# One ring of three buffers for the query weights and the second output projection, and the top-k ordered behind the second norm

## The chip, the core and the metric

The kernel runs on one core of one Trainium2 chip. A core has TensorE (PE, matrix products), VectorE (DVE), ScalarE (ACT), GpSimd (POOL) and SyncE (SP, which here only starts transfers). The metric is the device time of one execution in microseconds; lower is better.

## The reference, cut to what matters

```python
for l in range(DEPTH):                                    # DEPTH 1, x is (1, 512, 1024), f32
    proj = x @ w_in[l]                                    # 1024 -> 3072
    y_conv = gb * short_conv(gc * hc, conv_w[l], conv_b[l])
    y_att = rms_norm(diff_attention(q, k, v, lam), subln_g[l]) * (1.0 - lam_init)
    y_mix = jnp.concatenate([y_conv, y_att], axis=-1) @ w_out[l]
    x = layer_norm(DEEPNORM_ALPHA * x + y_mix, ln1_g[l], ln1_b[l])
    x = layer_norm(DEEPNORM_ALPHA * x + peer(x, ...), ln2_g[l], ln2_b[l])

def one_chunk(xc):                                        # in peer: 128 tokens
    q = (xc @ wq).reshape(128, 8, 2, 128)                 # 8 heads, two halves
    sc = jnp.einsum('chpd,hpnd->chpn', q, keys)           # 128 keys a half
    s1, i1 = lax.top_k(sc[:, :, 0], 16); s2, i2 = lax.top_k(sc[:, :, 1], 16)
    cand = s1[..., :, None] + s2[..., None, :]            # 256 candidates
    top_s, pos = lax.top_k(cand, 16)                      # 16 of 16384 experts a head
    g = jax.nn.softmax(top_s)
    act = jax.nn.gelu(jnp.einsum('chkd,cd->chk', u[eidx], xc))
    return jnp.einsum('chk,chkd->cd', g * act, v[eidx])
```

## The kernel before, in words

The 512 tokens are four chunks of 128. Every f32 weight block (128 x 1024, 512 KB) is loaded by SP's queue into a tile `raw` and split into a high part `whi` (a cast on ScalarE) and a low part `wlo` (a difference on VectorE or GpSimd); a product is then three matrix products, high by high, high by low and low by high (`mm3`, L89 to L91). `wblock` does the loading and splitting (L80 to L86), and its three tiles come from a pool: `raw` with three buffers, `whi` and `wlo` with the pool's own number, two in the pools `ws` and `ow`. A pool with n buffers is a ring: block n+1 can be split only when TensorE has read block 1.

After the input projection, the attention and the convolution come the stages around the change, in the program's text:

- `out_proj(0)`: the output projection of chunks 0 and 1, eight weight blocks of `w_out` from the pool `ws`, each with 12 products of 128x512; then, for each chunk, the first layer norm (L404 to L161), eight transposes on TensorE (L416), and the split of the transposed chunk into `x1Th` (ScalarE, L419) and `x1Tl` (VectorE, L420).
- `scores(0)`: 16 query blocks of `wq` from the pool `ws`, each with 24 products of 128x256 into `psH`, a copy `qT` on ScalarE (L444) and two small products with the keys (L452); the scores `sc` of chunks 0 and 1 stay in SBUF.
- `out_proj(1)`: the same for chunks 2 and 3, its blocks from the pool `ow`, with results in `x2Th` and `x2Tl` (L420).
- `scores(1)`: 16 more query blocks from `ws`; their scores go out to HBM (`SC_D`).
- `dense_u(j)`: blocks `uT` from `ws`, 24 products of 128x384 over chunks 0 to 2 and a GELU; blocks 0 to 19 take their low part on GpSimd, the others on VectorE.
- `topk` of chunks 0, 1 and 2 on VectorE (`top16`, L297 to L301, and `topk_rest`, L314 to L355), `gates` (softmax, L366 to L368), and their transposes on TensorE (L376 and L377). Chunk 2's scores are loaded back by SP's queue into a buffer that chunk 0's top-k frees.
- The one-hot stage (24 rounds, L532 to L544) builds the dense gates, with a dense_u block in each round; the last stage multiplies with `v`, while chunk 3 is done by gathering rows.

This text isn't the order of execution. A scheduler with its own estimate of times lays out every engine's instructions when the kernel is built, and hands out the buffers of a ring as it goes; `tc.issue_after(ins)` makes what is issued in its block come behind `ins` on the same engine. What each engine then has is a fixed order, in which every instruction waits for those ahead of it.

Of the kernel before, what the change touches and what calls it, by code (L numbers as in the profile page):

```python
# [9 lines left out]
F32 = mybir.dt.float32  # L10
F32R = mybir.dt.float32r
# [18 lines left out]
NDC = 3  # L30
# [26 lines left out]
def build(nc, tc, I, out, dbg=None):  # L57
# [3 lines left out]
    def load_pool(name, **kw):  # L61
        return tc.tile_pool(name=name, **kw)

    const = ctx.enter_context(load_pool("const", bufs=1, side="left"))
    ws = ctx.enter_context(load_pool("wstream", bufs=2, side="left"))
# [10 lines left out]
    def split(raw, hi, lo, sub):  # L76
        copied[0] = nc.scalar.copy(out=hi, in_=raw)  # L77
        return sub.tensor_sub(lo, raw, hi.bitcast(F32))  # L78

    def wblock(src, sub, pool=ws):  # L80
        raw = pool.tile([128, 8, 128], F32, name="raw", bufs=3)
        hi = pool.tile([128, 8, 128], F32R, name="whi")
        lo = pool.tile([128, 8, 128], F32R, name="wlo")
        nc.sync.dma_start(out=raw.rearrange("p a b -> p (a b)"), in_=src)
        split(raw, hi, lo, sub)
        return hi, lo  # L86

    def mm3(ps, lh, ll, rh, rl, first, last):
        nc.tensor.matmul(ps, lh, rh, start=first, stop=False)  # L89
        nc.tensor.matmul(ps, lh, rl, start=False, stop=False)  # L90
        return nc.tensor.matmul(ps, ll, rh, start=False, stop=last)  # L91
# [61 lines left out]
    def layernorm(xr, tot, gb, pool, junk):  # L153
        nm = pool.tile([128, 1], F32, name="lnnm", bufs=2)
        nc.vector.tensor_scalar(nm, tot, -1.0 / D, None, op0=ALU.mult)  # L155
        ss = pool.tile([128, 1], F32, name="lnss", bufs=2)
        nc.scalar.activation(junk, xr, AF.Square, bias=nm, accum_out=ss)
        nc.vector.scalar_tensor_tensor(xr, xr, nm, gb[0], op0=ALU.add, op1=ALU.mult)
        rs = pool.tile([128, 1], F32, name="lnrs", bufs=2)
        rsqrt_eps(rs, ss, 1.0 / D, pool)  # L160
        nc.vector.scalar_tensor_tensor(xr, xr, rs, gb[1], op0=ALU.mult, op1=ALU.add)  # L161
# [8 lines left out]
    wk = mix_ctx.enter_context(load_pool("wqtmp", bufs=2, side="right"))  # L170
# [54 lines left out]
    for h in range(NH):  # L225
# [11 lines left out]
        tp = psT.tile([128, S], F32, name="psT")  # L237
# [43 lines left out]
    tk = tk_ctx.enter_context(load_pool("topk", bufs=1, side="left"))  # L281
    iT = tk.tile([128, 2, ND, 2], F16, name="iT")
    gT = tk.tile([128, 2, ND, 2], F16, name="gT")
    scs = {}
    ow = mix_ctx.enter_context(load_pool("wout", bufs=2, side="right"))
# [9 lines left out]
    def top16(tk, vals, pos, src, n):  # L295
        t = tk.tile([128, 128], F32, name="rest", bufs=2)
        nc.vector.max(vals[:, 0:8], src)  # L297
        nc.vector.max_index(pos[:, 0:8], vals[:, 0:8], src)
        nc.vector.match_replace(t[:, 0:n], vals[:, 0:8], src, -3.0e38)  # L299
        nc.vector.max(vals[:, 8:16], t[:, 0:n])  # L300
        return nc.vector.max_index(pos[:, 8:16], vals[:, 8:16], t[:, 0:n])  # L301

    def topk(tk, sc, nb, between=None):
        m = tk.tile([128, 2, PH, 16], F32, name="m")
        ix = tk.tile([128, 2, PH, 16], U32, name="ix")
        for h in range(PH):
            for p in range(2):
                ins = top16(tk, m[:, p, h, :], ix[:, p, h, :], sc[:, 2 * h + p, :], 128)
        if between:
            with tc.issue_after(between(ins)):  # L310
                return topk_rest(tk, sc, nb, m, ix)
        return topk_rest(tk, sc, nb, m, ix)
# [72 lines left out]
    def out_proj(pair):  # L385
        acc = [psS.tile([128, 2, S], F32, name="psS") for _ in range(2)]
        for k in range(NK):
            hi, lo = wblock(I["w_out"][k * 128:(k + 1) * 128, :], nc.gpsimd if k % 2 else nc.vector, ow if pair else ws)
            hi, lo = hi.rearrange("p a b -> p (a b)"), lo.rearrange("p a b -> p (a b)")
            for j in range(2):  # L390
                cs = slice((2 * pair + j) * 128, (2 * pair + j + 1) * 128)
                for hf in range(2):
                    fs = slice(hf * 512, (hf + 1) * 512)
                    mm3(acc[j][:, hf, :], ych[:, k, cs], ycl[:, k, cs], hi[:, fs], lo[:, fs], k == 0, k == NK - 1)
        for j in range(2):
            c = 2 * pair + j
            if c == GCH:
                xr = x1
            else:
                xr = wk.tile([128, D], F32, name="xr")  # L400
            with tc.issue_after(y0.ins):
                nc.scalar.dma_start(out=xr, in_=I["x"][c * 128:(c + 1) * 128, :])
            tot = wk.tile([128, 1], F32, name="tot")
            nc.vector.scalar_tensor_tensor(xr, xr, ALPHA, acc[j].rearrange("p a b -> p (a b)"),  # L404
                                           op0=ALU.mult, op1=ALU.add, accum_out=tot)
            junk = wk.tile([128, D], F32, name="lnj", bufs=1)
            layernorm(xr, tot, (lnb[:, 0, :], lnb[:, 1, :]), wk, junk)
            if pair == 0:
                tps = [psT.tile([128, 4, 128], F32, name="psT") for _ in range(2)]
            else:  # L410
                tps = psS.tile([128, 2, S], F32, name="psS").rearrange("p a (k t) -> p a k t", k=4)
                tps = [tps[:, 0], tps[:, 1]]
            for g in range(2):
                tp = tps[g]
                for k in range(4):
                    nc.tensor.transpose(tp[:, k, :], xr[:, (4 * g + k) * 128:(4 * g + k + 1) * 128], ident)  # L416
                xs, cs = ((x1h, x1l), c) if pair == 0 else ((x2h, x2l), j)
                hi, lo = (t[:, 4 * g:4 * g + 4, cs * 128:(cs + 1) * 128] for t in xs)
                nc.scalar.copy(out=hi, in_=tp)  # L419
                nc.vector.tensor_sub(lo, tp, hi.bitcast(F32))  # L420
                if c == 2:
                    kept.append((g, hi, lo))
            if c != GCH:
                nc.scalar.dma_start(out=X1_D[c], in_=xr)

    kept = []

    def keep_chunk():
        for g, hi, lo in kept:
            for t, v in ((x1h, hi), (x1l, lo)):  # L430
                nc.scalar.copy(out=t[:, 4 * g:4 * g + 4, 256:384], in_=v.bitcast(F32))

    def scores(pair):
        if pair == 0:
            for c in range(2):
                scs[c] = tk.tile([128, 16, 128], F32, name="sc", bufs=2)
        xs_h, xs_l = (t[:, :, 0:256] for t in ((x2h, x2l) if pair else (x1h, x1l)))
        for hp_ in range(16):
            hi, lo = wblock(I["wq"][hp_], nc.gpsimd)
            ps = psH.tile([128, S], F32, name="psH")  # L440
            for k in range(NK):
                mm3(ps[:, 0:256], hi[:, k, :], lo[:, k, :], xs_h[:, k, :], xs_l[:, k, :], k == 0, k == NK - 1)
            qT = wk.tile([128, 256], F32, name="qT")
            nc.scalar.copy(out=qT, in_=ps[:, 0:256])  # L444
            if hp_ % 4 == 0:
                spp = [psT.tile([128, 4, 128], F32, name="psT") for _ in range(2)]
                ky = wk.tile([128, 4, 128], F32, name="ky")
                with tc.issue_after(y0.ins):
                    nc.scalar.dma_start(out=ky, in_=I["keysT"][:, hp_:hp_ + 4, :])
            for j in range(2):  # L450
                c = 2 * pair + j
                nc.tensor.matmul(spp[j][:, hp_ % 4, :], qT[:, j * 128:(j + 1) * 128], ky[:, hp_ % 4, :],  # L452
                                 start=True, stop=True)
                if hp_ % 4 == 3:
                    if pair == 0:
                        nc.scalar.copy(out=scs[c][:, hp_ - 3:hp_ + 1, :], in_=spp[j])
                    else:
                        st = wk.tile([128, 4, 128], F32, name="scst")
                        nc.scalar.copy(out=st, in_=spp[j])
                        nc.scalar.dma_start(out=SC_D[j][:, hp_ - 3:hp_ + 1, :], in_=st)  # L460

    out_proj(0)
    scores(0)
    out_proj(1)
    psS_ctx.close()
    g_ps = ExitStack()
    psG = g_ps.enter_context(tc.tile_pool(name="psG", bufs=4, space=PSUM))
    scores(1)
    keep_chunk()
    mix_ctx.close()  # L470
# [13 lines left out]
        hidden[j] = hs  # L484
        return mm, act

    picked = [topk(tk, scs[c], NDC) for c in range(2)]
    scs[2] = tk.tile([128, 16, 128], F32, name="sc", bufs=2)
    nc.sync.dma_start(out=scs[2], in_=SC_D[0])
    for j in range(GATES_AT[0]):  # L490
# [239 lines left out]
```

## Time and profile before

| | |
|---|---|
| median of three runs | 1506.69 us (1504.99 to 1508.18) |
| profiled execution | 1502.89 us |
| its span, first to last instruction | 1501.1 us |
| TensorE, products | 1456.8 us, 97% of the span |
| VectorE | 1183.6 us, 79% |
| ScalarE | 593.9 us, 40% |
| GpSimd | 477.9 us, 32% |
| mean granted TensorE clock | 0.988 |

The shares are means over stages with different limits. A wait counts only where it is on the way to the end; a TensorE that is called busy may still be running with a slow clock, so the granted clock is read beside it. Times in the text are microseconds from the start of the span; the stages named above lie between 185 and 605 us.

### The profile page before, as it was taken

What the parts mean: (1) busy time and instruction counts of PE and PEld (TensorE: products, weight loads), DVE (VectorE), ACT (ScalarE), POOL (GpSimd) and SP (SyncE); (2) the same over time, 40 slices, a digit from 0 to 9 for tenths busy, and PEclk for the clock granted to TensorE, in tenths of its full rate; (3) what the DMA queues carried; (4) which work ended last, traced back from release to release, by engine and by line L of the source; (5) the groups of instructions that cost most, each with busy time, mean ns of one, the idle gap of its engine ahead of it and who ended that gap; (6) DMA issues with size and microseconds to landing.
All of it is one profiled execution on the core that took longest, in us unless ns stands there. A gap on an engine that the chain in (4) does not pass through costs nothing.

```text
span 1501.1 us, 22151 instructions
## 1 busy us (share of the span) xinstructions
PE 1456.8 (97%) x8111; PEld 1307.0 (87%) x8111; DVE 1183.6 (79%) x2368; ACT 593.9 (40%) x937; POOL 477.9 (32%) x328
## 2 busy tenths in 40 slices
PE   9999988999988999899999999999999999999996
PEld 6777868999988999899998999998998999989875
DVE  4546455389997999599988888888888888888865
ACT  4443244543444555333433333333333333333342
POOL 1000043675640000000054444444444444444500
PEclk9999999999999999999999999999999999999998
DMA  4214264465425776989499999999999999999961
GB/s 172 71 57 155 85 212 144 154 204 186 126 98 186 264 262 258 301 267 270 136 349 378 329 348 342 342 344 334 339 321 355 328 340 344 328 339 329 329 222 70
DMA packets 146429, 375.94 MB, mean 250 GB/s; under 512 B 16272, under 2 KB 63376, under 8 KB 142992
## 3 DMA queue, kind: packets, MB, share of 16 engines
q1 hardware_dynamic: 100960, 203.97, 40.6%
q0 software_dynamic: 36864, 134.23, 24.7%
q10 hardware_dynamic: 8496, 36.32, 6.1%
q8 instruction: 63, 1.03, 0.3%
q14 instruction: 46, 0.38, 0.1%
HBM read 343.55 MB, written 30.93 MB: 249 GB/s over the span
## 4 chain that ended last, share of the span: by engine, by line
PE 79%; DVE 12%; DMA 4%; issue 2%; ACT 1%; POOL 1%; ACTq 0%; SPq 0%; POOLq 0%; DVEq 0%
PE psH L91 14%; PE psH L89 14%; PE psH L90 14%; PE acc L90 10%; PE acc L91 10%; PE acc L89 10%; DMA row<-v,idx 2%; PE psG L541 1%; PE psG L542 1%; PE psS L195 1%; DVE rest L299 1%; DVE sc L345 1%; POOL row L599 1%; DVE sc L353 1%; DMA raw<-w_out 1%
## 5 line engine op out<-in xcount | busy, mean ns | idle before, releaser
L77 ACT CAST whi<-raw 128x1024 fp32r<-128x1024 f32 x203 | 212.9, 1050 | 496.2 <-PE psH L90 362.6
L91 PE MATMUL psH<-x1Th,wlo 128*128 128x384 f32 (+1 forms) x1152 | 386.7, 336 | 13.4 <-DVE wlo L78 13.4
L89 PE MATMUL psH<-x1Th,whi 128*128 128x384 f32 (+1 forms) x1152 | 388.8, 338 | 2.9 <-ACT hs L483 1.9
L90 PE MATMUL psH<-x1Tl,whi 128*128 128x384 f32 (+1 forms) x1152 | 385.4, 335 | 0.0
L599 POOL DMA_INDIRECT row<-u,idx x128 | 162.9, 1272 | 486.7 <-DMA vr<-v 310.5
L90 PE MATMUL acc<-vl,wh 128*128 128x512 f32 x750 | 292.0, 389 | 1.5 <-DVE lnnm L155 1.5
L91 PE MATMUL acc<-vh,wl 128*128 128x512 f32 x750 | 291.8, 389 | 0.0
L89 PE MATMUL acc<-vh,wh 128*128 128x512 f32 x750 | 284.4, 389 | 0.0
L78 DVE TENSOR_TENSOR wlo<-raw,whi 128x1024 fp32r<-128x1024 f32 x143 | 176.6, 1235 | 100.2 <-ACT whi L77 83.7
L78 POOL TENSOR_TENSOR wlo<-raw,whi 128x1024 fp32r<-128x1024 f32 x60 | 146.7, 2447 | 285.9 <-ACT whi L77 285.0
L91 PEld LDWEIGHTS psH<-x1Th,wlo 128*128 128x128 f32 x1152 | 218.8, 190 | 14.4 <-DVE wlo L78 14.0
L89 PEld LDWEIGHTS psH<-x1Th,whi 128*128 128x128 f32 x1152 | 218.8, 190 | 6.9 <-ACT hs L483 2.3
L90 PEld LDWEIGHTS psH<-x1Tl,whi 128*128 128x128 f32 x1152 | 218.8, 190 | 3.0
L599 POOL DMA_INDIRECT row<-v,idx x128 | 163.2, 1275 | 180.0 <-DVE x L614 156.9
L77 ACT CAST wh<-hs 128x384 fp32r<-128x384 f32 x128 | 65.6, 514 | 317.0 <-PE acc L90 309.5
L614 DVE SCALAR_TENSOR_TENSOR x<-row,gw,x 128x1024 f32<-128x1024 f32 x128 | 163.7, 1279 | 7.1 <-DMA row<-v,idx 5.9
L91 PEld LDWEIGHTS acc<-vh,wl 128*128 128x128 f32 x750 | 140.8, 188 | 29.1
L90 PEld LDWEIGHTS acc<-vl,wh 128*128 128x128 f32 x750 | 140.8, 188 | 28.3 <-DVE vl L78 1.9
L89 PEld LDWEIGHTS acc<-vh,wh 128*128 128x128 f32 x750 | 140.8, 188 | 26.1
L78 DVE TENSOR_TENSOR vl<-vr,vh 128x1024 fp32r<-128x1024 f32 x125 | 152.5, 1220 | 13.9 <-ACT vh L77 10.9
L607 DVE SCALAR_TENSOR_TENSOR row<-row,x 128x1024 f32<-128x1024 f32 x128 | 154.3, 1218 | 9.5 <-DMA row<-u,idx 9.5
L77 ACT CAST vh<-vr 128x1024 fp32r<-128x1024 f32 x125 | 130.9, 1047 | 3.1 <-PE acc L91 3.1
(205 smaller groups left out, 1839.2 us busy)
## 6 DMA issues: line engine op xcount, KB each, us to landing
raw<-uT SPq DMA_DIRECT2D x128, 512.0 KB
vr<-v SPq DMA_DIRECT2D x125, 512.0 KB
G_D<-stg ACTq DMA_DIRECT2D x24, 1024.0 KB
gt<-G_D SPq DMA_DIRECT2D x46, 512.0 KB
raw<-wq SPq DMA_DIRECT2D x32, 512.0 KB
raw<-w_in SPq DMA_DIRECT2D x24, 512.0 KB
raw<-w_out SPq DMA_DIRECT2D x16, 512.0 KB
xr<-xT SPq DMA_DIRECT2D x4, 512.0 KB
```

The costliest lines, as they stand in the source:

```text
L77: copied[0] = nc.scalar.copy(out=hi, in_=raw)
L78: return sub.tensor_sub(lo, raw, hi.bitcast(F32))
L89: nc.tensor.matmul(ps, lh, rh, start=first, stop=False)
L90: nc.tensor.matmul(ps, lh, rl, start=False, stop=False)
L91: return nc.tensor.matmul(ps, ll, rh, start=False, stop=last)
L195: nc.tensor.matmul(sp[:, p, 0:w], qz[:, h, p, qs], kT[:, h, 0:w], start=True, stop=False)
L299: nc.vector.match_replace(t[:, 0:n], vals[:, 0:8], src, -3.0e38)
L345: nc.vector.tensor_tensor(e[:, p].rearrange("p a (n e) -> p a n e", e=2), ab[:, p].rearrange("p k h -> p (k h)").rearrange("p (n e) -> p n ...
L353: nc.vector.tensor_tensor(e[:, :, 0:n], e[:, :, 0:n], e[:, :, n:2 * n], op=ALU.add)
L599: ins = nc.gpsimd.indirect_dma_start(out=t, out_offset=None, in_=I["uv"[p]], in_offset=bass.IndirectOffsetOnAxis(ap=idx[:, p, k:k + 1], ax ...
L607: nc.vector.scalar_tensor_tensor(t, t, 1.0, x1, op0=ALU.mult, op1=ALU.mult, accum_out=dots[:, k:k + 1])
L614: nc.vector.scalar_tensor_tensor(x1, t, gw[:, k:k + 1], x1, op0=ALU.mult, op1=ALU.add, accum_out=tots[:, GCH:GCH + 1] if k == 127 else None)
```

## The change

`wblock` gets an argument for the number of buffers of `whi` and `wlo`. The query blocks of both halves move from `ws` to `ow`, where out_proj(1)'s blocks already were, and the ring there gets three buffers; `qT` gets one buffer instead of two. The last difference that out_proj makes (L420) is remembered in `normed`, and the top-k of chunks 0 and 1 is ordered behind it on VectorE.

```diff
-    def wblock(src, sub, pool=ws):
+    def wblock(src, sub, pool=ws, bufs=2):
         raw = pool.tile([128, 8, 128], F32, name="raw", bufs=3)
-        hi = pool.tile([128, 8, 128], F32R, name="whi")
-        lo = pool.tile([128, 8, 128], F32R, name="wlo")
+        hi = pool.tile([128, 8, 128], F32R, name="whi", bufs=bufs)
+        lo = pool.tile([128, 8, 128], F32R, name="wlo", bufs=bufs)
...
     def out_proj(pair):
...
-            hi, lo = wblock(I["w_out"][...], nc.gpsimd if k % 2 else nc.vector, ow if pair else ws)
+            hi, lo = wblock(I["w_out"][...], nc.gpsimd if k % 2 else nc.vector, *((ow, 3) if pair else (ws,)))
...
-                nc.vector.tensor_sub(lo, tp, hi.bitcast(F32))
+                normed[0] = nc.vector.tensor_sub(lo, tp, hi.bitcast(F32))
...
     def scores(pair):
...
-            hi, lo = wblock(I["wq"][hp_], nc.gpsimd)
+            hi, lo = wblock(I["wq"][hp_], nc.gpsimd, ow, 3)
...
-            qT = wk.tile([128, 256], F32, name="qT")
+            qT = wk.tile([128, 256], F32, name="qT", bufs=1)
...
-    picked = [topk(tk, scs[c], NDC) for c in range(2)]
+    with tc.issue_after(normed[0].ins):
+        picked = [topk(tk, scs[c], NDC) for c in range(2)]
```

The diff doesn't show what the scheduler makes of it. The numbers in the following rows tell buffers' uses apart. TensorE, at the end of out_proj(0) (`psS_1540`), before; `psS_2341` is out_proj(1):

```order
L89 MATMUL psS_1540<-whi_1668,ych_157 128x512
L90 MATMUL psS_1540<-wlo_1669,ych_157 128x512
L91 MATMUL psS_1540<-whi_1668,ycl_158 128x512
L89 MATMUL psS_2341<-whi_2344,ych_157 128x512
L90 MATMUL psS_2341<-wlo_2345,ych_157 128x512
L91 MATMUL psS_2341<-whi_2344,ycl_158 128x512
```

and after, where `psT` are the transposes of the normed chunks 0 and 1 and `psH_1763` is the first query block:

```order
L89 MATMUL psS_1540<-whi_1668,ych_157 128x512
L90 MATMUL psS_1540<-wlo_1669,ych_157 128x512
L91 MATMUL psS_1540<-whi_1668,ycl_158 128x512
L416 MATMUL psT_1705<-ident_125,xr_1685 128x128 x4
L416 MATMUL psT_1706<-ident_125,xr_1685 128x128 x4
L416 MATMUL psT_1740<-ident_125,xr_1720 128x128 x4
L416 MATMUL psT_1741<-ident_125,xr_1720 128x128 x4
L89 MATMUL psH_1763<-x1Th_1523,whi_1758 128x256
```

Before, four blocks of out_proj(1) stood between out_proj(0) and the first of these transposes, and query blocks between out_proj(1) and its own. Now TensorE has the transposes right behind the products that the norm needs, in both places, and all 16 query blocks of scores(0) stand ahead of out_proj(1).

GpSimd's splits at the same place, before; 1597, 1633 and 1669 are blocks 3, 5 and 7 of out_proj(0), 2363 is out_proj(1)'s, 1759 and 1798 the first query blocks:

```order
L78 TENSOR_TENSOR wlo_1561<-raw_1559,whi_1560 128x1024
L78 TENSOR_TENSOR wlo_1597<-raw_1595,whi_1596 128x1024
L78 TENSOR_TENSOR wlo_2363<-raw_2361,whi_2362 128x1024
L78 TENSOR_TENSOR wlo_1633<-raw_1631,whi_1632 128x1024
L78 TENSOR_TENSOR wlo_1669<-raw_1667,whi_1668 128x1024
L78 TENSOR_TENSOR wlo_1759<-raw_1757,whi_1758 128x1024
```

and after, with 1833 the third query block and 3513 and 3546 the first two of dense_u:

```order
L78 TENSOR_TENSOR wlo_1561<-raw_1559,whi_1560 128x1024
L78 TENSOR_TENSOR wlo_1759<-raw_1757,whi_1758 128x1024
L78 TENSOR_TENSOR wlo_1597<-raw_1595,whi_1596 128x1024
L78 TENSOR_TENSOR wlo_1798<-raw_1796,whi_1797 128x1024
L78 TENSOR_TENSOR wlo_1833<-raw_1831,whi_1832 128x1024
L78 TENSOR_TENSOR wlo_1633<-raw_1631,whi_1632 128x1024
L78 TENSOR_TENSOR wlo_1669<-raw_1667,whi_1668 128x1024
L78 TENSOR_TENSOR wlo_3513<-raw_3511,whi_3512 128x1024
L78 TENSOR_TENSOR wlo_3546<-raw_3544,whi_3545 128x1024
```

Three query blocks' splits now stand among those of out_proj(0), where one of out_proj(1) stood, and two of dense_u's come long before they are used.

VectorE at the end of the second norm (L161), before:

```order
L161 SCALAR_TENSOR_TENSOR x_141<-x_141,lnrs,ln1gb 128x1024
L297 MAX m<-sc 128x8 x4
L420 TENSOR_TENSOR x2Tl<-psS,x2Th 128x4x128
L298 MAX_INDEX ix<-m,sc 128x8
L299 MATCH_REPLACE rest<-m,sc 128x128
```

and after:

```order
L161 SCALAR_TENSOR_TENSOR x_141<-x_141,lnrs,ln1gb 128x1024
L420 TENSOR_TENSOR x2Tl<-psS,x2Th 128x4x128 x4
L297 MAX m<-sc 128x8 x13
L298 MAX_INDEX ix<-m,sc 128x8
L299 MATCH_REPLACE rest<-m,sc 128x128
```

The four differences of the second norm now stand ahead of the whole top-k instead of among its first operations.

More of the change, by code (lines that the diff above doesn't have):

```diff
@@ L387, in out_proj @@
         for k in range(NK):
-            hi, lo = wblock(I["w_out"][k * 128:(k + 1) * 128, :], nc.gpsimd if k % 2 else nc.vector, ow if pair else ws)
+            hi, lo = wblock(I["w_out"][k * 128:(k + 1) * 128, :], nc.gpsimd if k % 2 else nc.vector, *((ow, 3) if pair else (ws,)))
             hi, lo = hi.rearrange("p a b -> p (a b)"), lo.rearrange("p a b -> p (a b)")
@@ L426, in build @@
     kept = []
+    normed = [None]
     def keep_chunk():
```

## The prediction

> **What bounds the kernel now.** I read the page's span and its chain, then a table of busy times by stretch, then the list of waits, and last the order of time around the waits that this change touches.
>
> ```profile
> span 1501.1 us, 22151 instructions
> PE 79%; DVE 12%; DMA 4%; issue 2%; ACT 1%; POOL 1%; ACTq 0%; SPq 0%; POOLq 0%; DVEq 0%
> ```
>
> The chain is TensorE (PE) for four fifths and VectorE (DVE) for an eighth. Where that eighth lies, the stretches tell (columns: from:to, length, then busy us and instructions of each engine, granted clock, DMA):
>
> ```profile
> core 0: us, PE busy (x) PEld busy (x) DVE busy (x) ACT busy (x) POOL busy (x), PEclk, DMA share, GB/s
> 260.00:353.20 93.20, 93.20 (x782) 92.82 (x781) 64.42 (x275) 45.70 (x75) 65.12 (x27) 0.98 0.58 187
> 353.20:369.60 16.40, 14.45 (x77) 14.13 (x76) 16.40 (x75) 6.44 (x9) 7.89 (x5) 0.90 0.57 198
> 369.60:443.80 74.20, 74.18 (x423) 73.79 (x421) 73.75 (x297) 31.74 (x49) 40.28 (x16) 1.00 0.37 120
> 443.80:454.40 10.60, 0.08 (x1) 0.08 (x1) 10.56 (x16) 2.36 (x3) 0.00 (x0) 0.66 0.00 0
> 454.40:605.00 150.60, 150.60 (x1350) 146.96 (x1351) 133.64 (x118) 81.04 (x145) 0.00 (x0) 0.99 0.68 249
> ```
>
> From 353 to 454 VectorE has no idle time: that is the top-k. TensorE runs beside it and then stands still from 443.8 to 454.4, because dense_u block 20 is the first whose low half VectorE makes, and that split stands behind the whole top-k:
>
> ```profile
> PE psH L91 <- DVE wlo L78: 10.5, 1, 10.5
> ...
> 454.32 0.69 PE L91 MATMUL psH<-x1Th,wlo 128*128 128x384 f32 x1 [10.54 <-DVE wlo L78]
> ```
>
> From 454.4 on TensorE is busy without a gap (150.60 of 150.60). All five engines' orders are the same in both kernels from dense_u block 2 on (VectorE's from the end of the top-k), but for one load on SP's queue (step 6). So the question is one number: when VectorE and TensorE reach that split in the new order; whatever it moves, the rest of the kernel moves with it.
>
> **The change, part by part.** The order shows that the code does more than its words. The queries' blocks and the second output projection now share one ring, and the ring is filled in program order: all 16 query blocks of the first half (scores(0)) come ahead of out_proj(1). Before, out_proj(1) filled TensorE during the first norm, and scores(0) filled it during the second. Now both norms have nothing beside them, and the top-k can't begin before the second is done.
>
> *Step 1, end of out_proj(0).* GpSimd (POOL) now splits three query blocks between the blocks of out_proj(0), where before it split one.
>
> ```profile
> 194.94 4.79 POOL L78 TENSOR_TENSOR wlo<-raw,whi 128x1024 fp32r<-128x1024 f32 x2 [6.16 <-ACT whi L77]
> 197.44 0.50 PE L90 MATMUL psS<-wlo,ych 128*128 128x512 f32 x1 [1.79 <-POOL wlo L78]
> 213.65 0.39 PE L91 MATMUL psS<-whi,ycl 128*128 128x512 f32 x1
> ```
>
> TensorE waits for such a split at 197.44. One more of 2.4 us ahead of it, and the one after follows from it, since the ring of two lets the next block be split only when TensorE is done with one. I take 2.5 us; bounds 0 (hidden by the loads) and 4.8 (two splits). out_proj(0) then ends at 214.0 + 2.5 = 216.5.
>
> *Step 2, the first norm.* It is now bare on TensorE.
>
> ```profile
> 220.19 1.23 DVE L78 TENSOR_TENSOR wlo<-raw,whi 128x1024 fp32r<-128x1024 f32 x1
> 221.51 2.45 DVE L150 SCALAR_TENSOR_TENSOR rsq_t<-rsq_t,rsq_a 128x1 f32<-128x1 f32 x2
> 223.89 0.27 DVE L151 SCALAR_TENSOR_TENSOR lnrs<-rsq_t,lnrs 128x1 f32<-128x1 f32 x2
> 225.41 1.09 PE L416 MATMUL psT<-ident,xr 128*128 128x128 f32 x8 [0.89 <-DVE xr L161]
> 226.96 1.08 ACT L419 CAST x1Th<-psT 128x512 fp32r<-128x512 f32 x2
> 228.05 1.28 DVE L420 TENSOR_TENSOR x1Tl<-psT,x1Th 128x512 fp32r<-128x512 f32 x2
> 246.91 0.39 PE L91 MATMUL psS<-whi,ycl 128*128 128x512 f32 x1
> 258.76 0.63 PE L416 MATMUL psS<-ident,xr 128*128 128x128 f32 x4 [3.21 <-DVE rsq_t L149]
> ```
>
> In both norms the transposes start 11.4 us after the last product (225.4 - 214.0; 258.8 - 247.3). Without the weight split at 220.19 (1.2) and with L150 at its free length (its 2.45 lies in a GpSimd split; two such tiny operations take 0.27 in the row of L151) 8.1 are left, and 8.6 with a new split of GpSimd's that can fall on an operation of it. I take 8.6; bounds 7 (an estimate: nothing in it held up by GpSimd) and 11.4. Then come transposes, cast, difference, transposes of the other chunk, cast (halves of the rows above): 3.4 us to the first query product. Together 12.0.
>
> *Step 3, clock.* After such idle time the granted clock falls:
>
> ```profile
> 250.00:260.00 10.00, 6.14 (x49) 5.75 (x48) 8.59 (x12) 5.03 (x11) 4.84 (x2) 0.98 0.34 107
> 260.00:270.00 10.00, 10.00 (x76) 10.00 (x75) 7.67 (x37) 6.86 (x13) 4.72 (x2) 0.85 0.42 132
> ```
>
> 0.02 and 0.15 of 10 us are 1.7 us lost, behind a wait of 3.2. I take 1.7 for each norm; bound 3.4. The Trainium skill (TensorE: Matmul & The Clock Gate, What's actually happening) has the clock at half after an idle window of about 3.4 us until a busy one; the trace agrees in kind, and by that rule a norm would cost 1.7 to 3.4.
>
> *Step 4, scores(0) and out_proj(1).* Four recorded rows of line 452 make a query block, so this stretch has 24 blocks, 3.30 us each:
>
> ```profile
> 273.90:353.15 79.25, 14.56 (x96) 12.76 (x97) 1.00 0.61 197
> 214.54 0.39 PE L90 MATMUL psS<-wlo,ych 128*128 128x512 f32 x1
> 219.20 0.39 PE L89 MATMUL psS<-whi,ych 128*128 128x512 f32 x1
> ```
>
> TensorE is busy throughout them (93.20 of 93.20 above), so the third buffer has nothing to remove there: I give it 0, bounds 0 and -2. The single qT buffer costs 0: the copy of one block has a whole block of products to finish in. 16 blocks are 52.8 us. In out_proj(1) 20 products start within 4.66 us, 0.233 each; 96 of them are 22.4.
>
> *Step 5, the second norm, and where the top-k starts.* 8.6 to the transposes, then casts and copies on ScalarE and four differences on VectorE, 5.5 (7 casts or copies of 0.6 and the last difference of 0.65): 14.1. The top-k starts at 216.5 + 12.0 + 1.7 + 52.8 + 22.4 + 14.1 = 319.5.
>
> *Step 6, the top-k.* From 260 to 454.4 the stretches hold 165.1 us of VectorE; less the four differences (2.6), the norm's rest (0.5) and the split itself (1.3), 160.8 are the work ahead of the split. Before, 61 of these were done by 353, in the shadow of the queries; now all of it follows 319.5. No wait falls inside: the scores of chunks 0 and 1 are long there, and chunk 2's are written by about 375, its load freed at about 380 and needed at about 400. That load now stands ahead of dense_u block 5's on SP's queue, which so comes some microseconds late, for an engine that will have to wait anyway. Part of the work is collisions with GpSimd:
>
> ```profile
> 347.98 3.38 DVE L349 TENSOR_TENSOR sc<-sc,ixf 128x2048 f16<-128x2048 f16 x1
> ...
> 353.13 1.57 DVE L353 TENSOR_TENSOR sc<-sc 128x2048 f16<-128x2048 f16 x1
> ...
> 355.02 2.48 DVE L353 TENSOR_TENSOR sc<-sc 128x1024 f16<-128x1024 f16 x1
> ...
> 435.74 0.74 DVE L341 TENSOR_TENSOR ab<-ix 128x128 f16<-128x128 uint32 x1
> ...
> 439.50 1.23 DVE L349 TENSOR_TENSOR sc<-sc,ixf 128x2048 f16<-128x2048 f16 x1
> ...
> L345 DVE TENSOR_TENSOR sc<-ab,iota 128x2048 f16<-128x2048 f16 x6 | 13.4, 2226 | 0.1
> L349 DVE TENSOR_TENSOR sc<-sc,ixf 128x2048 f16<-128x2048 f16 x6 | 11.6, 1940 | 0.1
> ...
> L340 DVE SCALAR_TENSOR_TENSOR ix<-pos,ix 128x128 uint32<-128x128 uint32 x3 | 7.4, 2480 | 0.0
> L341 DVE TENSOR_TENSOR ab<-ix 128x128 f16<-128x128 uint32 x3 | 6.6, 2204 | 0.0
> L337 DVE SCALAR_TENSOR_TENSOR ab<-ix 128x128 f16<-128x128 uint32 x3 | 6.4, 2125 | 0.1
> ```
>
> L349 takes 1.23 where GpSimd is idle and 3.38 where it splits. In these five groups the surplus is 6 x 1.0 + 6 x 0.7 + 13.7 (20.4 less 9 x 0.74) = 24 us. In the new order the last query split ends near 364, and the next ones follow TensorE's dense_u blocks from 375, so the last three operations of the first top-k (the first three rows) run free: I take 5.4 off; bounds 0 and 24. So 155.4 us, and the split starts at 474.9 instead of 453.05: **+21.9**.
>
> *Step 7, TensorE's own arrival.* Its scores(1) begin at 305.4 + 11.3 = 316.7 and end at 371.2; 14 dense_u blocks later (60.0, as from 353.6 to 417.2 less the 1.95 idle and the tenth of the clock in the stretch from 353.2) it is at 431 and wants the first chunk's gates.
>
> ```profile
> L368 DVE TENSOR_TENSOR g<-gx,gs x2: 411/425/439, 416.4 to 416.6; 128x128 f32<-128x128 f32 x2
> L376 PE MATMUL psT<-ident,idf x4: 270/272/272, 417.2 to 421.9; 128*128 128x128 f32 x4
> ```
>
> Before, gates and transposes met (416.9, 417.2). Now the gates come 119 us after 319.5, at 439: a new wait of 8 us. 26.6 us of blocks and a slow clock bring TensorE to 467, where it waits another 8 for the split. The old wait of 10.5 is thus split in two and made longer, and the top-k sets the restart. The idle 1.95 of that stretch goes (dense_u blocks 0 and 1 are now split early), but is swallowed by these.
>
> **Sum.** The profiled execution took 1502.89 us (span 1501.1): 1524.8 after. The median of the runs is 1506.69, 3.8 above that execution, so I forecast 1506.7 + 22 = **1529 us**.
>
> **Rivals.**
> - *The norms stay as long as they are.* 11.4 each (+5.6), the clock's upper bound (+1.7), GpSimd's second split (+2.3) and no collision saved (+5.4): about +35, 1541. For it: both norms took 11.4, in both some operation stood in a GpSimd split. Against it: the weight split inside is gone.
> - *The collisions vanish,* the one that can end on the other side. Place: the top-k's operations with two inputs in SBUF, and the norms. The rows say 24 us. Then VectorE would arrive at 456 or sooner, and TensorE decides, with 20.7 blocks of 4.28 from 371.2 and no gates to wait for: 459.8, or 454 with both norms at 7 and step 1 hidden. Against its restart at 454.3 that is 0 to +6, 1507 to 1513; it is no slower (under +3) from the point where the top-k falls under 138 us and that arrival under 457. Against it: 18 dense_u blocks are still split by GpSimd beside the top-k, 16 starts within 369.6 to 443.8 in the table. The Trainium skill (SBUF — State Buffer, Who interferes with whom) says that such an operation and a GpSimd one that reads SBUF block each other entirely; the trace agrees (3.38 against 1.23), and by it the price hangs on how many splits are left.
> - *The third buffer speeds the queries:* at most 2 us of step 4, and the top-k follows later all the same: inside my range.
>
> **Chances.** The forecast's case, +11 to +33: 0.75. Long norms: 0.13. Collisions gone or nearly so: 0.12, half of it within or under 0.2% (3 us, about what a measurement of this kernel tells from no change). So slower 0.94, same 0.04, faster 0.02. The range is the forecast's with the nearer part of the long norms: step 2 and 5 give -3 and +6, step 6 -9 and +5, step 1 and 3 -3 and +4: 1516 to 1541.
>
> **What the profile would show.** Two bare waits of TensorE of 10 to 13 us near 217 and 306, each followed by a low clock; the first MAX8 near 320 with VectorE then without idle time; a wait of 5 to 11 at the gates' transposes; the split near 475. I am wrong if VectorE reaches it before 465 (collisions) or if TensorE gets there last.

## The result, and the profile after

The changed kernel takes 1521.46 us in the median (four runs, 1519.91 to 1522.89), the kernel before in the same comparison 1505.84 (four runs, 1502.14 to 1508.18). The ratio is 1.0105, 95% interval 1.0088 to 1.0122: 15.6 us slower, where +22 was forecast. The profiled execution of after took 1522.89 us, 1.4 above its median; that of before took 1502.89, 3.0 below its own. So the spans differ by 20.0 and the medians by 15.6, and a landmark of these two traces is good to some microseconds only.

The span, the chain, and TensorE's waits from 190 to 480 (releaser, then us in total, times, longest):

```profile
span 1521.1 us, 22163 instructions
PE 82%; DVE 11%; DMA 2%; issue 2%; ACT 1%; POOL 1%; ACTq 0%; SPq 0%; POOLq 0%; DVEq 0%
```
```profile
PE psH L91 <- DVE wlo L78: 11.5, 1, 11.5
PE psT L416 <- DVE xr L161: 8.3, 1, 8.3
PE psS L416 <- DVE xr L161: 8.3, 1, 8.3
PE psS L90 <- POOL wlo L78: 4.1, 3, 3.1
PE psT L377 <- DVE g L368: 0.9, 1, 0.9
```

The two bare norms are there, 8.3 us each, where before there were waits of 0.9 and 3.2 at the same transposes. The wait for the split of dense_u block 20 is still one piece, and a microsecond longer. The gates cost 0.9. The way to the restart as a table (from:to, length, busy us of PE, PEld, DVE, ACT, POOL with instructions, granted clock, DMA):

```profile
216.25:228.85 12.60, 3.73 (x17) 3.00 (x17) 9.45 (x23) 5.62 (x10) 2.47 (x2) 0.65 0.53 183
228.85:306.16 77.31, 77.31 (x545) 72.27 (x544) 7.39 (x7) 33.01 (x48) 44.78 (x19) 0.97 0.51 165
306.16:320.49 14.33, 5.70 (x32) 4.96 (x32) 10.73 (x25) 8.34 (x15) 3.13 (x2) 0.64 0.38 129
320.49:381.40 60.91, 60.31 (x484) 59.79 (x482) 60.85 (x306) 25.05 (x41) 34.95 (x15) 1.00 0.41 137
381.40:433.72 52.32, 51.41 (x290) 51.03 (x290) 52.25 (x252) 21.52 (x30) 30.27 (x13) 1.00 0.40 137
433.72:460.24 26.52, 26.52 (x150) 26.03 (x150) 26.35 (x82) 11.57 (x22) 13.02 (x5) 1.00 0.33 113
460.24:471.70 11.46, 0.00 (x0) 0.00 (x0) 11.43 (x17) 2.38 (x3) 0.00 (x0) 0.59 0.00 0
471.70:622.30 150.60, 150.60 (x1340) 146.97 (x1341) 133.76 (x118) 80.47 (x145) 0.00 (x0) 0.99 0.67 248
```

From top to bottom: the first norm up to the first query product; scores(0) and out_proj(1) in one piece; second norm; scores(1); 14 dense_u blocks; six more; the wait; and then the same 150.60 us without a gap that stood behind the restart before. From 320 to 471.7 VectorE is as good as never idle: that is the top-k, and two rows mark its ends:

```profile
320.49 1.64 DVE L297 MAX8 m<-sc 128x8 f32<-128x128 f32 x8
...
470.43 1.22 DVE L78 TENSOR_TENSOR wlo<-raw,whi 128x1024 fp32r<-128x1024 f32 x1
```

The restart is at 471.70 against 454.32, +17.4. Behind it the distance stays at 17.4 to 17.7 us until the last 65 us of the span, where after loses 2.3 more (a wait of 2.3 in place of 1.5, and slow products behind it).

### The profile page after: what moved, and what is told of

Read it like the earlier page. It is cut to its first block, busy times and chain, and to the rows that moved or that the text cites. A ratio compares the mean times of both kernels' runs of the same rounds, so it can differ in the third digit from the quotient of the medians.

```text
span 1521.1 us, 22163 instructions
## 1 busy us (share of the span) xinstructions
PE 1461.5 (96%) x8111; PEld 1310.6 (86%) x8111; DVE 1167.7 (77%) x2368; ACT 595.0 (39%) x937; POOL 481.2 (32%) x328
## 4 chain that ended last, share of the span: by engine, by line
PE 82%; DVE 11%; DMA 2%; issue 2%; ACT 1%; POOL 1%; ACTq 0%; SPq 0%; POOLq 0%; DVEq 0%
PE psH L89 14%; PE psH L91 14%; PE psH L90 14%; PE acc L90 11%; PE acc L91 11%; PE acc L89 11%; PE psG L543 1%; PE psG L544 1%; PE psS L195 1%; DVE rest L299 1%; DVE ix L301 1%; DVE ix L298 1%; POOL wlo L78 1%; DMA row<-v,idx 1%; DVE m L300 1%
```

## The experiments

Every time is compared with the kernel before on the same chip (medians of 1506.1 to 1507.3). Theory A is the prediction's: the bare norms put off the top-k, and the top-k sets the restart. Its rivals are in the expectations.

**One part alone: the rings, and the order.** The first kernel is the changed one without the top-k's order:

```diff
-    with tc.issue_after(normed[0].ins):
-        picked = [topk(tk, scs[c], NDC) for c in range(2)]
+    picked = [topk(tk, scs[c], NDC) for c in range(2)]
```

> The changed kernel without the order behind the second norm: the shared ring of three stays, the top-k is free. Theory A (the restart at dense_u block 20 is set by the start of the top-k plus its work, and the start by the two norms that nothing covers): VectorE now begins the top-k beside scores(0), near 240, and is done with it long before 454; TensorE's own arrival decides, which in the changed kernel was 460.2 less the 0.9 at the gates, so the restart comes near 459 to 463, +5 to +9 on the kernel before: 1510 to 1515. Rival B (TensorE's bare norms alone are the price, whoever waits for the top-k): still +16, 1521. Rival C (the order behind the norm is the price): back to 1506.

1521.17 us (four runs), ratio 1.0112 (1.0096 to 1.0127): the whole loss, so this expectation of theory A failed, and the number is rival B's. The second is the kernel before with the order and nothing else:

> The kernel before with only the order of the top-k behind the second norm. Theory A: TensorE's order is as before, both norms are covered, the last difference comes near 263 and the top-k waits for the scores of the first half until about 307 as it did; restart 452 to 457, 1504 to 1508. Rival C (the order itself is the price): +10 or more, above 1516.

1505.84 us (eleven runs), ratio 0.9995 (0.9982 to 1.0007): by the medians the order by itself costs nothing. The one trace missed the expected landmarks: the top-k begins at 274.78, where before it began at 260.31, and the restart is at 462.18 and not at 452 to 457. That execution took 1511.03 us, the longest of the eleven and 5.2 above their median, so it doesn't speak against the median, and where it lost the time is open. The loss belongs to the ring, which takes all of scores(0) ahead of out_proj(1).

Why didn't an early top-k help? In the ring's kernel it begins at 248, 72 us sooner than in after, and yet the split comes at the same 470.55. VectorE's waits between 380 and 475, and then TensorE's longest three between 190 and 480, say why:

```profile
DVE gs L366 <- ACT gx L361: 16.1, 1, 16.1
DVE m L297 <- DMA sc<-SC_D: 11.0, 1, 11.0
```
```profile
PE psS L416 <- DVE lnrs L151: 11.9, 1, 11.9
PE psT L416 <- DVE xr L161: 8.3, 1, 8.3
PE psH L91 <- DVE wlo L78: 4.8, 1, 4.8
```

The first two top-ks are done at 380, but chunk 2's scores come only out of scores(1), behind both norms (11.0 us of waiting for their reload). Then the first gates, which the code puts inside the third top-k and behind dense_u block 9's GELU on ScalarE, hold VectorE for 16.1 more. VectorE can be early only with the chunks whose scores are there; its last third goes by TensorE's position. On the other side the top-k's operations, now free, got in among the second norm's: 11.9 us in place of 8.3, and a long stretch at half clock behind it:

```profile
320.00:330.00 10.00, 8.20 (x39) 7.19 (x38) 10.00 (x36) 3.62 (x7) 0.00 (x0) 0.59 0.00 0
```

TensorE itself arrived at 467.0 (471.83 less 4.8), not near 460 as in after, and 23 later than in before (443.8). So rival B holds in part: with the bare norms TensorE alone would be late by the whole loss. The order does one thing here, it keeps the second norm at 8.3, and pays for it with a top-k that starts late: the sum is the same.

**The bare norms undone, the rest kept.** The changed kernel with two lines exchanged, so that the second projection is ahead of the first queries in the ring:

```diff
     out_proj(0)
-    scores(0)
     out_proj(1)
+    scores(0)
```

> The changed kernel with out_proj(1) written ahead of scores(0), so that the ring of three is filled with out_proj(1) first; the top-k stays behind the second norm. Theory A: out_proj(1) covers the first norm and scores(0) the second, no wait of 8 us is left, the top-k starts near 262 and is fed by scores(0) until about 307; restart 450 to 456, 1502 to 1508. Rival C (the order itself): +10 or more. Rival D (the third buffer is worth something where the queries run): 1495 to 1501.

1498.09 us (five runs), ratio 0.9953 (0.9939 to 0.9966): 23 us better than after, and 8 better than before. It was faster than theory A had it; the number is rival D's, and the next part asks how much of it is owed to the third buffer. TensorE's waits between 190 and 480, first of this kernel, then (to 460) of before, the four longest each:

```profile
PE psH L91 <- DVE wlo L78: 10.5, 1, 10.5
PE psS L90 <- POOL wlo L78: 2.6, 3, 1.8
PE psS L90 <- DVE wlo L78: 1.4, 1, 1.4
PE psS L416 <- DVE rsq_t L150: 1.2, 1, 1.2
```
```profile
PE psH L91 <- DVE wlo L78: 10.5, 1, 10.5
PE psS L416 <- DVE rsq_t L149: 3.2, 1, 3.2
PE psS L90 <- POOL wlo L78: 2.6, 3, 1.8
PE psH L89 <- ACT hs L483: 1.9, 1, 1.9
```

Both norms are covered, and the two waits of before that were followed by a low clock, 3.2 and 1.9, are down to 1.2 and 0.6 (the 0.6 is the fifth of the list). Two stretches of each kernel, before first:

```profile
260.00:280.00 20.00, 20.00 (x159) 19.83 (x158) 8.20 (x40) 11.79 (x21) 10.83 (x5) 0.93 0.45 142
360.00:380.00 20.00, 18.05 (x94) 17.73 (x93) 19.93 (x125) 6.90 (x9) 8.64 (x4) 0.91 0.47 164
```
```profile
260.00:280.00 20.00, 20.00 (x173) 20.00 (x172) 10.14 (x65) 10.77 (x19) 14.38 (x6) 1.00 0.57 186
360.00:380.00 20.00, 20.00 (x115) 20.00 (x114) 19.90 (x71) 5.99 (x9) 11.47 (x5) 1.00 0.39 132
```

Ahead of block 20 the whole lists sum to 11.1 us in before and 6.5 in this kernel, and the clock rows give 20 x (0.07 + 0.09) = 3.2 more: 7.8 us, which is what TensorE's arrival moved (435.98 against 443.78). But the restart is set by VectorE's split, in both kernels 10.5 us behind that arrival, so VectorE must have come sooner too. The last thing that its top-k waits for are scores that TensorE makes (before first):

```profile
305.93 0.87 DVE L297 MAX8 m<-sc 128x8 f32<-128x128 f32 x4 [8.40 <-ACT sc L456]
```
```profile
300.19 0.87 DVE L297 MAX8 m<-sc 128x8 f32<-128x128 f32 x4 [8.31 <-ACT sc L457]
```

They are there 5.7 us sooner, and from there to the split VectorE takes 145.1 us in place of 147.1; no run shows where these 2.1 went. The restart is at 446.52 against 454.32.

**The third buffer.** First the changed kernel, then the one with the two lines exchanged, each with two buffers in the ring, `(ow, 2)` in place of `(ow, 3)` at both calls:

> The changed kernel with two buffers in the shared ring in place of three; all else, the order of the code and the top-k's place among it, as changed. Theory A (the third buffer is worth nothing, since TensorE has no idle time in its query blocks): the changed kernel's time within 2 us, 1519 to 1523, query period 3.26 to 3.32 us, restart of dense_u block 20 at 471 to 473. Rival D (the third buffer is worth something where queries and second projection run, and the price of the bare norms is larger than 16 us): 1524 to 1529, with idle time of TensorE among the query blocks.

1532.25 us (five runs), ratio 1.0172 (1.0148 to 1.0196): 11 us slower than after, and neither theory had that much. D's sign, idle time of TensorE among the query blocks, is there (below).

> The swapped kernel (second output projection written ahead of the first half's queries, which measured 1498.1) with two buffers in the shared ring in place of three. Theory A (its gain over the kernel before comes from the order of the ring alone: the second projection fills the first norm and the queries fill the second, each without a gap): 1497 to 1500. Rival D (the third buffer lets GpSimd run ahead across the norms, and gives the 8 us): 1503 to 1508, with waits of TensorE for a weight's low half at the norms or behind them.

1500.36 us (twelve runs), ratio 0.9965 (0.9951 to 0.9978): at the edge of what theory A expected: 2.3 us more than with three, with intervals that overlap. So in the good order most of the gain over before (6.4 of 8.0 us, each against its own before) doesn't need the third buffer, and in the order of the change it is worth 11 us. What it is worth in the good order stays open, though. In the trace with two buffers TensorE waits three times for a low half of a query block (2.1 us in all), as rival D expected, and the restart is at 452.57, 6 us later than with three; behind the restart that execution took 4.4 us less, for a reason that no run shows. Fourteen query blocks of the first half, with two buffers and then with three:

```profile
237.39:287.61 50.22, 47.49 (x388) 46.20 (x389) 1.23 (x1) 20.41 (x33) 31.31 (x14) 1.00 0.49 163
```
```profile
237.03:283.25 46.22, 46.22 (x395) 46.13 (x395) 1.23 (x1) 21.42 (x34) 33.31 (x14) 1.00 0.54 177
```

Both rows are of the changed order. That is 3.59 us a block against 3.30, and 2.7 of the 4.0 are idle time. One place in it, with two buffers, and ScalarE's copy that it waits for:

```profile
250.47 0.61 PE L453 MATMUL psT<-ky,qT 128*128 128x128 f32 x4
...
251.97 0.71 PE L453 MATMUL psT<-ky,qT 128*128 128x128 f32 x4 [0.65 <-ACT qT L445]
```
```profile
251.55 0.37 ACT L445 COPY qT<-psH 128x256 f32<-128x256 f32 x1
```

With two buffers the scheduler set every fourth block's score products 1.5 us behind the last ones, right after that block's own products, where the copy of qT isn't done; with three they come once a block, a full block later. So in the query blocks it is mostly the order on TensorE that cost the time (eight such waits sum to 4.9 us), and little a block that came late (1.2 us for low halves); the single qT buffer, the same in both, shows only where a copy is asked for at once. But the restart, at 482.96, is set by VectorE, whose top-k has these two ends:

```profile
326.98 2.60 DVE L297 MAX8 m<-sc 128x8 f32<-128x128 f32 x13
...
481.69 1.22 DVE L78 TENSOR_TENSOR wlo<-raw,whi 128x1024 fp32r<-128x1024 f32 x1
```

It starts 6.5 us later than in after, which the slower query blocks of the first half can explain for the most part (16 x 0.29 = 4.6), and then takes 154.7 us in place of 149.9 without a wait inside. Single groups move both ways (six operations of L345 from 9.5 to 13.5 us, six of L349 from 9.5 to 7.3), as they would if the collisions with GpSimd's splits fell on other operations; no run separates this. What three buffers give to out_proj(1) in a ring of its own wasn't tried.

**GpSimd's splits taken away beside the top-k.** In the changed kernel dense_u blocks 0 to 19 use the high part in place of the low one, so their difference on GpSimd is left out:

```diff
+        if sub is None:
+            copied[0] = nc.scalar.copy(out=hi, in_=raw)
+            return hi, hi
...
-        uh, ul = wblock(I["uT"][j], nc.gpsimd if j < NPOOL else nc.vector)
+        uh, ul = wblock(I["uT"][j], None if j < NPOOL else nc.vector)
```

> The changed kernel, but dense_u blocks 0 to 19 use their high part in place of the low one and GpSimd makes no split for them (a part of the computation is left out). Theory A with collisions (VectorE loses time wherever an operation with two inputs meets a GpSimd split): about 14 us of the 149.9 that the top-k took fall after 375 and go; VectorE is at the split near 456 and TensorE's own arrival, 459 to 461, decides: restart 10 to 12 sooner than 471.7, 1509 to 1513. Rival: collisions are not what lengthens those operations: 1519 to 1523.

1505.72 us (eleven runs), ratio 1.0001 (0.9992 to 1.0010): 16 us less than after, more than expected. Two of the five groups of the prediction, first in after, then here (lines three further down, the mean in ns behind the comma):

```profile
L345 DVE TENSOR_TENSOR sc<-ab,iota 128x2048 f16<-128x2048 f16 x6 | 9.5, 1589 | 0.1
L340 DVE SCALAR_TENSOR_TENSOR ix<-pos,ix 128x128 uint32<-128x128 uint32 x3 | 6.0, 2001 | 0.0
```
```profile
L348 DVE TENSOR_TENSOR sc<-ab,iota 128x2048 f16<-128x2048 f16 x6 | 7.3, 1219 | 0.1
L343 DVE SCALAR_TENSOR_TENSOR ix<-pos,ix 128x128 uint32<-128x128 uint32 x3 | 3.1, 1020 | 0.0
...
457.89 1.22 DVE L78 TENSOR_TENSOR wlo<-raw,whi 128x1024 fp32r<-128x1024 f32 x1
```

VectorE starts the split at 457.9, 12.5 us sooner than in after, and TensorE (459.2) no longer waits there; both arrive together, with the two bare norms still in place (7.6 and 8.3). Since TensorE hasn't stood still, it also goes on at the full clock. The first 4 us from that point, first in after, then here:

```profile
471.70:475.70 4.00, 4.00 (x12) 4.00 (x13) 1.80 (x4) 0.00 (x0) 0.00 (x0) 0.50 0.66 193
```
```profile
459.20:463.20 4.00, 4.00 (x24) 4.00 (x24) 1.23 (x1) 1.42 (x3) 0.00 (x0) 1.00 0.48 147
```

The first one-hot product comes 14.4 us sooner (467.40 against 481.81), so a wait at block 20 costs some 2 us more than its length. The last 1.9 of the 16.3 between the two traces fall behind that. The prediction named "no slower" for a top-k under 138 us and an arrival of TensorE under 457. The top-k took 138.1, TensorE came at 459.2, as the rival had it (459.8), and the time is that of before.

**What is left of the top-k in the better order.** NPOOL 23 in place of 20 gives three more splits to GpSimd, first with the two lines exchanged, then in the kernel before:

```diff
-NPOOL = 20
+NPOOL = 23
```

> The swapped kernel with NPOOL 23 in place of 20: GpSimd splits dense_u blocks 20 to 22 too, so that VectorE's first split behind the top-k is that of block 23. Theory A (the wait of 10.5 us at block 20 is what is left of the top-k; TensorE reaches block 23 at about 436 + 13 = 449, VectorE's top-k ends at 445 to 449): the wait falls to 0 to 2, 1487 to 1491. Rival (the three splits more collide with the top-k's operations and put off its end by as much as they save): wait of 4 to 10 at block 23, 1493 to 1499.

1491.90 us (six runs), ratio 0.9912 (0.9889 to 0.9935), between the two expectations and the best of all: 6 us less than with 20, and 15 less than before. The wait didn't vanish. It moved to the one-hot stage, whose operands stand behind the same top-k, and that now ends some 9 us later beside the added splits:

```profile
449.30 0.22 PE L543 MATMUL psG<-bh,oa 128*128 128x128 f16 x1 [2.60 <-DVE bh L536]
452.57 0.27 PE L544 MATMUL psG<-bl,oa 128*128 128x128 f16 x1 [3.06 <-DVE bl L537]
```

> The kernel before with NPOOL 23 in place of 20, nothing else. Theory A (the wait of 10.5 us at block 20 goes, since TensorE reaches block 23 at 444 + 13 = 457 and the top-k ends at 453 to 456): 1494 to 1498. Rival (the added splits put off the top-k): 1500 to 1507. In both the time tells what the end of the top-k, and not TensorE's own work, costs in the kernel before.

1501.11 us (twelve runs), ratio 0.9963 (0.9950 to 0.9976): 5 to 6 us gained, inside the rival's range and short of theory A's, although the wait at block 20 is gone. Here 3.1 and 0.6 us stand at the one-hots, and a wait of 3.5 at the transposes of the first chunk's gates is new. Both runs say that of the 10.5 us at block 20 about half can be had in this way; the rest comes back as waits for VectorE at other places.

**The order where the norms are covered.** The exchanged kernel without the `issue_after`:

> The swapped kernel (1498.1) without the top-k's order: the first two top-ks may stand ahead of the second norm on VectorE. Theory A (the order is worth nothing where a norm has TensorE work beside it): 1496 to 1500, first MAX8 ahead of 262, restart of block 20 within 3 us of 446.5. Rival (the top-k's operations get in among the second norm's, as where only the rings were changed, and the norm's 3 to 4 us more come out at TensorE, half clock included): 1501 to 1507, with a wait of TensorE of 4 us or more at the second norm's transposes.

1497.67 us (six runs), ratio 0.9947 (0.9929 to 0.9965): the same as with it. The second norm's wait is 1.6 and the restart at 448.32. But the order hardly binds here: without it the top-k begins at 262.28 and not 262.86, a little later than expected, because its first scores aren't there sooner (a wait of 1.4 for them). So the rival's case, a top-k among the norm's operations, didn't arise, and the run shows only that nothing is lost without the order. The run that moves the start of the top-k, by 14.5 us, is the one of the kernel before with the order alone, and its median is unchanged too.

## Why the prediction was right, step by step, and where a size was off

*Step 1 and 2* held. out_proj(0) ended at 216.25 (forecast 216.5), with a wait of 3.1 for one split. The norms' waits were 8.32 and 8.31 (8.6). From the end of the products to the first query product it took 12.60 (12.0), 0.9 of it more in the first eight transposes, which ran at a clock of 0.50 (1.94 where before it was 1.09).

*Step 3*, the clock, was a little small for the first norm. The first of these rows, from the first query product on, lacks 0.46 of 5.15 us, which is 2.4 us and not 1.7; then the clock is full:

```profile
228.85:234.00 5.15, 5.15 (x25) 4.93 (x25) 1.36 (x2) 0.59 (x1) 0.00 (x0) 0.54 0.22 76
234.00:306.16 72.16, 72.16 (x522) 67.35 (x521) 6.03 (x5) 32.43 (x47) 44.78 (x19) 1.00 0.53 172
```

Behind the second it cost nothing on its own: the slow products (0.64 in the table's third row) were the transposes, which lie inside the 14.33 that the norm took (14.1). The Trainium skill (TensorE: Matmul & The Clock Gate, What's actually happening) gives the clock back only after a whole busy window of about 3.4 us, which the prediction turned into an estimate of 1.7 to 3.4 lost; the 2.4 agrees. But behind the 11.9 us norm of the ring's kernel the clock was still at 0.59 through 320 to 330: there the first products came with gaps of 0.4 to 0.9 us, and the full rate (0.28 us a product, 0.41 before that) came back at 328, 10 us behind the first of them. In after it came back at 233.4, 9 us behind the first transposes. That the gaps kept it down isn't shown.

*Step 4* held: 3.30 us a query block, and no idle time. "The third buffer: 0" was right as a difference from the kernel before, whose blocks ran at the same rate with two. As a worth of the buffer inside this change it was wrong by 11 us, as the run with two in the shared ring shows. The rival that the buffer speeds the queries didn't come about: they were no faster than before.

*Step 5*: the top-k began at 320.49 (319.5). The terms up to there missed by -0.3, +0.6, +0.4 (clock, queries and second projection together) and +0.2 us, so this landmark is not one that errors in both directions made.

*Step 6* is the term that was mis-sized. From 320.49 to 470.43 it took 149.9 us, where 155.4 were forecast: of the 160.8 of before, 10.9 went and not 5.4. The prediction took off only the three operations that would fall between the last query split and the first dense_u split, and left every other collision as it was. In the five groups the row sums fall from 45.4 to 35.9, and the halving products of L353 lose another 2. Which splits meet an operation of two inputs hangs on microseconds of phase: with two buffers in the ring, the same top-k took 154.7. So 5.4, the one gap that could be named, was a term of no great certainty; its bounds of 0 and 24 held. The Trainium skill (SBUF — State Buffer, Who interferes with whom) has such an operation and a GpSimd split exclude each other for a whole instruction; the run without those splits agrees (L340's mean of 2.00 falls to 1.02). In after it is 18 such splits beside the top-k, 11.9 us of 149.9, that make it the last to arrive.

*Step 7* failed in its first half: the gates wait was 0.9 and not 8. The gates came at 433.3 and not 439, for the reason of step 6, and TensorE at 432.8 and not 431, so they met as they had before. The wait at the split was 11.5 and not 8, so that the sum hardly changed. That the top-k sets the restart held (460.24 against 471.70).

Sum: the split came at 470.43 (474.9), which is 4.5 of the 7.5 us between 1529 and 1521.5. Another 0.9 is that before measured 1505.84 and not 1506.69. The other 2 are the scatter of single executions: the restart moved by 17.4 in the traces and the medians by 15.6. Of the rivals, long norms didn't come (8.3, not 11.4); the vanishing of the collisions is what the run without GpSimd's splits made by hand, and it gave a time at the rival's near end (no change). What the prediction did not see is that the top-k's late start was not the only thing that put off the restart: without its order, TensorE by itself arrives at 467, and VectorE's last third is still at the split at 470.6.

## What to carry to other kernels

A shared ring of buffers is an ordering: blocks are split in program order, so moving a stage's weights into another stage's ring can take away the work that covered a serial step elsewhere. Look in the order at what stands beside each serial step (here a norm) before counting buffers; here exchanging two lines turned 1% slower into 0.5% faster, and three more splits on GpSimd into 0.9%. An earlier start of one engine shows nothing if its last piece still waits for another, as in the ring's kernel; ask what that piece waits for.

## What the runs showed that was not expected

Going from three buffers to two changed less when blocks arrive than how the scheduler ordered TensorE: about 0.3 us a query block over the first half's blocks, and a top-k that was 4.8 us longer behind them. A wait of TensorE's at block 20 also costs about 2 us of slow clock behind it. And a wait that is removed comes back one stage on if its releaser comes no sooner: of the 10.5 us at block 20, 5.7 stood again at the one-hots.
